# Order of the turned rows' parts, the place of the last turn, and the PSUM banks of the second down pass in a Griffin-style encoder layer

## The chip, the cores and the metric

The kernel runs on one core of a Trainium2 chip. The metric is the device time of one execution in microseconds (us); lower is better. One core has TensorE (matmuls; its rows in the profile are PE, and PEld for the loads of the stationary operand), VectorE (DVE), ScalarE (ACT), GpSimd (POOL) and SyncE (SP, which here issues DMAs). The on-chip memories are SBUF and PSUM; TensorE writes its results to PSUM, which has eight banks.

## The reference

One layer of a bidirectional hybrid encoder on 512 rows of 1024 float32 numbers. What matters here is its second half:

```python
x1 = x + rmsnorm(merged @ w_out, g_post_mix)
h2 = rmsnorm(x1, g_pre_ffn)
hid = conv3(h2 @ w_up) + conv_b            # w_up: 1024 x 5632, conv of width 3 along the rows
a, b = split(hid)                          # 2816 columns each
y = x1 + rmsnorm((gelu(a) * b) @ w_down, g_post_ffn)   # w_down: 2816 x 1024
```

The first half (a retention branch, a gated branch and their gates) makes `merged`; the change does not touch it.

## The kernel before, in words

**Precision.** Every matmul operand is held as two parts: a high part, which ScalarE copies into a reduced float32 type, and a low part, which VectorE makes by subtracting the high part from the original. A product is three matmuls: high by high, high by low, low by high. Where the original itself is needed later, a third copy, the raw rows, is made.

**Order.** The program is traced in Python, and a planner then puts the instructions of each engine in one fixed order at build time, from its own estimate of when each is ready, with earlier-traced ones first; it also hands out the buffers, PSUM banks among them, and sets the waits. So the order on an engine need not be that of the source. `tc.issue_after(ins)` forces instructions traced inside the block to stand behind `ins` on its engine. A PSUM bank is one tile from `ps()`; two engines' accesses to one bank are put one after the other, also when both only read.

**The turn.** `Down` computes `merged @ w_out` into eight accumulators, two for each of four row tiles t of 128 rows, and `finish(t, n)` adds the last six of eight blocks for one half n. `norms(t, acc)` makes the first norm and the residual x1 of row tile t, sends x1 out by DMA, and makes the rows of the second norm (`xn`, L873) from a scale (`row_scale`: L837 on DVE, L840 on POOL). `turn(t, zs)` transposes these rows on TensorE (L886, eight 128-column matmuls into two banks, one for each n), and evacuates each bank in two halves i: high parts (`h2h`, ACT), raw rows (`h2r`, ACT) and low parts (`h2l`, DVE, L892). Turns 0 and 1 fill group 0 (rows 0 to 255, the slice T0), turns 2 and 3 group 1 (T1).

Turn t-2 stands between the two `finish` calls of row tile t. After the loop, four blocks of the up projection start early: `early(e, 0)` is block e on T0 (24 matmuls of 256 columns, L219 to L221), `early(e, 1)` the same on T1. Turn 2 stands after `early(0, 0)`, turn 3 after `early(3, 0)`, right ahead of `early(0, 1)`, which is the first to read group 1. Then the rest of the up projection follows (plain blocks by L219 to L221, and a Strassen form of pairs by L673 that uses sums of the raw rows, L911 to L914), with conv and gate.

**The down projection** runs twice, once for each half of the 1024 output columns, in a Strassen-Winograd form: seven products M1, M2, M3, M5, M6, M7, M4 in this order, each in a PSUM bank of its own, accumulated over nine steps j; M8 is an eighth bank. In the last step of the first pass the `steps` functions combine the banks on VectorE into `c11` to `c22` as each product ends. The second pass takes new tiles from `ps()`, so each gets a bank of the first pass that has been read. On DVE the same stretch also holds the preparation of the next weights (L185, L189, L190 sums; L87 low parts `dl`).

Of the kernel before, what the change touches and what calls it, by code (L numbers as in the profile page):

```python
# [19 lines left out]
KD = D // P  # L20
# [28 lines left out]
def tile_block(ctx: ExitStack, tc, xT, x, wall, par, cs, wsp, bsp, gpost, gpre, gffn, out):  # L49
# [23 lines left out]
    def ps(shape=(P, S)):  # L73
        return pp.tile(list(shape), F32, tag="ps", name=nm("ps"))
# [4 lines left out]
    def copy(o, i):  # L79
        nc.scalar.activation(out=o, in_=i, func=AF.Copy)  # L80

    def as32(t):
        return t.bitcast(F32)
# [750 lines left out]
    def row_scale(q):  # L834

        s_, o = small("qs", 1, 4), small("qr", 1, 4)
        i = v.scalar_tensor_tensor(  # L837
            out=s_, in0=q[:, 0:1], scalar=EPS, in1=q[:, 1:2], op0=ALU.add, op1=ALU.add
        )
        nc.gpsimd.tensor_tensor(out=o, in0=s_, in1=nhalf[:, 0:1], op=ALU.pow)  # L840
        return o, i
# [7 lines left out]
    def norms(t, acc):  # L849

        xt = halves("x1")
        for n in range(2):
            nc.sync.dma_start(xt[n], x[t, :, n * S : (n + 1) * S])
        q = small("q", 2, 4)
        for n in range(2):
            mean_square(q, n, acc[n])
        sc, _ = row_scale(q)
        q = small("q", 2, 4)
        for n in range(2):
            z = tmp("z")  # L860
            v.scalar_tensor_tensor(
                out=z, in0=acc[n], scalar=sc, in1=gpm[n], op0=ALU.mult, op1=ALU.mult
            )
            v.tensor_add(xt[n], xt[n], z)
            mean_square(q, n, xt[n])
            nc.gpsimd.dma_start(x1[t][n], xt[n])
            if n == 0 and t in ADDED:
                nc.gpsimd.dma_start(out[t, :, 0:S], xt[0])
        sc, _ = row_scale(q)
        zs = []  # L870
        for n in range(2):
            z = tmp("xn")
            v.scalar_tensor_tensor(  # L873
                out=z, in0=xt[n], scalar=sc, in1=gpf[n], op0=ALU.mult, op1=ALU.mult
            )
            zs.append(z)
        return zs
# [2 lines left out]

    def turn(t, zs):
        g, c = t // 2, slice((t % 2) * P, (t % 2 + 1) * P)
        for n in range(2):
            p = ps()
            for f in range(4):
                nc.tensor.transpose(p[:, f * P : (f + 1) * P], zs[n][:, f * P : (f + 1) * P], ident)  # L886
            for i in range(2):
                hi, lo, raw = (h[g][2 * n + i].rearrange(two, i=2)[:, :, c] for h in (h2h, h2l, h2r))
                pf = p[:, 2 * i * P : 2 * (i + 1) * P].rearrange(two, i=2)
                copy(hi, pf)  # L890
                copy(raw, pf)
                v.tensor_sub(lo, pf, as32(hi))  # L892

    def h2(k, t):
        f = slice((k % 2) * 256, (k % 2 + 1) * 256)
# [19 lines left out]
        for n, t in zip(("S1", "S2", "S3", "S4"), (b1, a0, a1, b0)):  # L915
            h2_parts(n, i, t)

    def h2_block(w, o, q):
        wh, wl = w
        for k in range(KD):  # L920
            c = slice(k * P, (k + 1) * P)
            mm3(o[:, q], wh[:, c], wl[:, c], *h2(k, q), k == 0, k == KD - 1)

# [7 lines left out]

    early_w, early_o = [], []

    def early(e, q):

        if q == 0:
            early_w.append(w_get(1))
            early_o.append(ps())
        h2_block(early_w[e], early_o[e], (T0, T1)[q])

    dn_ = Down(mh, ml, KD, RES_OUT)
    zs = {}
    for t in range(NT):
        acc = [dn_.finish(t, 0)]
        if t > 1:
            turn(t - 2, zs[t - 2])
        acc.append(dn_.finish(t, 1))
        zs[t] = norms(t, acc)
    early(0, 0)
    turn(2, zs[2])  # L950
    for e in range(1, EARLY):
        early(e, 0)
    turn(3, zs[3])
    for e in range(EARLY):
        early(e, 1)

# [84 lines left out]
    def products(m, j, steps={}):  # L1041
        for n, (unit, at, act) in enumerate(UNITS):
            if n in (0, 3):
                wh, wl = w_get()
            if j == 0:
                m[n] = ps()
            f = slice(at * 256, (at + 1) * 256)
            ah, al = dforms[j][act]
            for t in range(2):
                c = slice(t * P, (t + 1) * P)  # L1050
                o = m[n][:, t * 256 : (t + 1) * 256]
                for i, (a_, w_) in enumerate(((ah, wh), (ah, wl), (al, wh))):
                    nc.tensor.matmul(  # L1053
                        o, a_[:, c], w_[:, f], start=j == t == i == 0,
                        stop=j == DP - 1 and i == 2 and n not in (M2, M3, M4), skip_group_check=True,
                    )
            steps.get(n, lambda: None)()
# [21 lines left out]
    c11, c12, c21, c22 = c4 = [blk(n="c") for _ in range(4)]  # L1079
    e1, e3, uu, yy = tmp("e1"), tmp("e3"), tmp("uu"), tmp("yy")  # L1080

    def after6():
        v.tensor_add(uu, m[M6], e1)
        v.tensor_sub(c12, m[M5], uu)
        v.tensor_add(c12, c12, e3)

    def after7():
        v.tensor_add(e1, m[M7], uu)
        v.tensor_sub(yy, m[M5], e1)  # L1089
        v.tensor_add(c22, c22, yy)  # L1090

    steps = {
        M1: lambda: copy(e1, m[M1]),
        M2: lambda: v.tensor_add(c11, m[M2], e1),
        M3: lambda: copy(e3, m[M3]),
        M6: after6, M7: after7,
        M4: lambda: v.tensor_add(c21, m[M4], e1),
    }
    for j in range(DP):
        if j < WHOLE:  # L1100
# [22 lines left out]
        v.tensor_add(qn[t][:, 0:1], qn[t][:, 2:3], qn[t][:, 3:4])  # L1123


    m = {}
    e1, uu, xx, yy = (blk(n="e") for _ in range(4))

    def after6():
# [10 lines left out]
        if 1 < j < 2 + NT:  # L1140
            first_share(j - 2)
    ww = [w_get(), w_get()]
    m[M8] = ps()

    def rows(t, sc, z, xt, some=(0, 1, 2)):

# [170 lines left out]
```

## Time and profile before

| | us |
|---|---|
| median of 3 runs | 829.89 |
| lowest and highest run | 827.95, 831.93 |
| the profiled execution, its own time | 832.1 |
| span of that execution, first to last instruction | 830.3 |
| PE busy in the span | 819.6 |
| PEld busy | 760.9 |
| DVE busy | 659.3 |
| ACT busy | 430.9 |
| POOL busy | 104.4 |

The mean granted TensorE clock is 0.998. Times in a timeline are counted from the span's start. A row of the timeline has the start, the duration, engine, line, operation, what is written from what, and in brackets the idle time of that engine before it and what ended it. TensorE is pipelined: a matmul's duration in a row is longer than the distance from its start to the next one's start, so the pace of TensorE is read from starts, or from the number of matmuls in a window.

### The profile page before, as it was taken

What the parts mean: (1) busy time and instruction counts of PE and PEld (TensorE: products, weight loads), DVE (VectorE), ACT (ScalarE), POOL (GpSimd) and SP (SyncE); (2) the same over time, 40 slices, a digit from 0 to 9 for tenths busy, and PEclk for the clock granted to TensorE, in tenths of its full rate; (3) what the DMA queues carried; (4) which work ended last, traced back from release to release, by engine and by line L of the source; (5) the groups of instructions that cost most, each with busy time, mean ns of one, the idle gap of its engine ahead of it and who ended that gap; (6) DMA issues with size and microseconds to landing.
All of it is one profiled execution on the core that took longest, in us unless ns stands there. A gap on an engine that the chain in (4) does not pass through costs nothing. (4 is left out here: it accounts for less than half of the span.)

```text
span 830.3 us, 14356 instructions
## 1 busy us (share of the span) xinstructions
PE 819.6 (99%) x5728; PEld 760.9 (92%) x5728; DVE 659.3 (79%) x1076; ACT 430.9 (52%) x733; POOL 104.4 (13%) x108
## 2 busy tenths in 40 slices
PE   9999999999999999999999999999999999999996
PEld 7888888888899999999988899999999999999995
DVE  7489898877897777767765679679899789997956
ACT  6635445546665444444444456456566566644532
POOL 0010000102221111133221201111111100000002
PEclk9999999999999999999999999999999999999999
DMA  8733222213233333233459121333323341243344
GB/s 279 258 115 104 75 77 77 76 52 99 69 102 126 102 102 93 87 100 102 121 178 349 64 67 37 105 104 99 116 91 101 110 147 50 77 141 103 115 128 127
DMA packets 29251, 93.84 MB, mean 113 GB/s; under 512 B 3392, under 2 KB 4032, under 8 KB 29184
## 3 DMA queue, kind: packets, MB, share of 16 engines
q1 hardware_dynamic: 26784, 86.58, 32.6%
q0 software_dynamic: 1968, 6.03, 2.3%
q8 instruction: 45, 0.74, 0.4%
q10 hardware_dynamic: 432, 0.30, 0.1%
q14 instruction: 22, 0.18, 0.1%
HBM read 88.19 MB, written 4.72 MB: 112 GB/s over the span
## 5 line engine op out<-in xcount | busy, mean ns | idle before, releaser
L87 DVE TENSOR_TENSOR wl<-raw,wh 128x1024 fp32r<-128x1024 f32 (+1 forms) x93 | 109.4, 1186 | 50.8 <-PE ps L673 27.3
L80 ACT ACTIVATE wf<-raw 128x512 fp32r<-128x512 f32 x140 | 85.3, 626 | 102.8 <-PE ps L220 45.0
L87 DVE TENSOR_TENSOR wf<-raw,wf 128x512 fp32r<-128x512 f32 x140 | 109.2, 795 | 26.8 <-ACT wf L80 25.9
L220 PE MATMUL ps<-h2l,wh 128*128 128x256 f32 x448 | 124.6, 279 | 0.2 <-DVE h2l L892 0.2
L219 PE MATMUL ps<-h2h,wh 128*128 128x256 f32 x448 | 123.7, 278 | 0.0
L221 PE MATMUL ps<-h2h,wl 128*128 128x256 f32 x448 | 123.7, 277 | 0.0
L673 PE MATMUL ps<-sh,wf 128*128 128x256 f32 x640 | 120.2, 277 | 0.1
L80 ACT ACTIVATE wh<-raw 128x1024 fp32r<-128x1024 f32 (+2 forms) x95 | 93.0, 989 | 35.9 <-DMA raw<-wall 13.3
L673 PEld LDWEIGHTS ps<-sh,wf 128*128 128x128 f32 x640 | 101.3, 188 | 0.8 <-DVE c L701 0.3
L673 PE MATMUL ps<-sl,wf 128*128 128x256 f32 x320 | 89.1, 278 | 0.0
L220 PEld LDWEIGHTS ps<-h2l,wh 128*128 128x128 f32 x448 | 83.9, 187 | 0.7 <-DVE h2l L892 0.7
L219 PEld LDWEIGHTS ps<-h2h,wh 128*128 128x128 f32 x448 | 83.8, 188 | 0.3 <-ACT h2h L80 0.3
L221 PEld LDWEIGHTS ps<-h2h,wl 128*128 128x128 f32 x448 | 83.9, 188 | 0.0
L481 PE MATMUL ps<-wh,xh 128*128 128x512 f32 x192 | 75.0, 391 | 0.0
L482 PE MATMUL ps<-wl,xh 128*128 128x512 f32 x192 | 74.9, 390 | 0.0
L483 PE MATMUL ps<-wh,xl 128*128 128x512 f32 x192 | 74.8, 390 | 0.0
L168 POOL TENSOR_TENSOR raw<-raw,raw 128x512 f32<-128x512 f32 x20 | 35.1, 1755 | 239.9 <-DVE raw L166 212.5
L1053 PE MATMUL ps<-dh,fh 128*128 128x256 f32 x216 | 60.9, 282 | 0.3 <-DVE yy L1089 0.2
L1053 PE MATMUL ps<-dh,fl 128*128 128x256 f32 x216 | 60.9, 282 | 0.0
L673 PEld LDWEIGHTS ps<-sl,wf 128*128 128x128 f32 x320 | 60.0, 188 | 0.3
L1053 PE MATMUL ps<-dl,fh 128*128 128x256 f32 x216 | 60.3, 279 | 0.0
L673 PE MATMUL ps<-xh,wf 128*128 128x256 f32 x288 | 54.4, 279 | 0.0
(309 smaller groups left out, 2040.1 us busy)
## 6 DMA issues: line engine op xcount, KB each, us to landing
raw<-wall SPq DMA_DIRECT2D x145, 512.0 KB, 3.6
x<-x SPq DMA_DIRECT2D x22, 256.0 KB, 5.5
xT<-xT SPq DMA_DIRECT2D x8, 256.0 KB, 5.4
x<-x POOLq DMA_DIRECT2D x8, 256.0 KB, 2.4
xT<-xT POOLq DMA_DIRECT2D x4, 256.0 KB, 3.8
out<-zs SPq DMA_DIRECT2D x3, 256.0 KB, 3.3
cs<-cs SPq DMA_DIRECT2D x2, 256.0 KB, 4.0
gpm<-gpost POOLq DMA_DIRECT2D x2, 256.0 KB, 3.8
```

The source lines that it names most:

```text
L80: nc.scalar.activation(out=o, in_=i, func=AF.Copy)
L87: nc.vector.tensor_sub(lo, src, as32(hi))
L168: nc.gpsimd.tensor_tensor(out=w_raw["T2"], in0=w_raw["T1"], in1=w_raw["B22"], op=ALU.add)
L219: nc.tensor.matmul(o, ah, bh, start=start, stop=False)
L220: nc.tensor.matmul(o, ah, bl, start=False, stop=False)
L221: nc.tensor.matmul(o, al, bh, start=False, stop=stop)
L481: nc.tensor.matmul(acc[t], xh[k][:, c], wh[:, f], start=k == 0, stop=False)
L482: nc.tensor.matmul(acc[t], xh[k][:, c], wl[:, f], start=False, stop=False)
L483: nc.tensor.matmul(acc[t], xl[k][:, c], wh[:, f], start=False, stop=k == KD - 1)
L673: nc.tensor.matmul(o, w_[:, c], a_, start=first and k == n == 0, stop=k == 3 and n == 2, skip_group_check=True,)
L1053: nc.tensor.matmul(o, a_[:, c], w_[:, f], start=j == t == i == 0, stop=j == DP - 1 and i == 2 and n not in (M2, M3, M4), skip_group_check= ...
```

## The change

Five edits:

1. In `turn`, the four raw copies on ScalarE are traced after all high and low parts of both banks, instead of each between its high and its low part; `turn` returns its last low part.
2. `norms` is split: its last part, the second scale and the two products by it (L837, L840, two L873), becomes `scaled(xt, q)`. For row tile 2 alone it is not traced at the end of `norms` but in the next round, after turn 1, and forced behind turn 1's last low part on DVE. For the other tiles it stays where it was. The DMAs of `norms` (x1, and part of the output) stay.
3. Turn 3 moves from the end of `early(3, 0)` to its middle, after 12 of its 24 matmuls.
4. In the first down pass, `c12 = M5 - uu` moves from after M6 to after M7, behind `yy = M5 - e1`; `c12 + e3` and `c22 + yy` move behind M4's `c21`.
5. The second pass gets its eight banks by name instead of from `ps()`: M1 the first pass's M8, M2 its M1, M3 its M2, M5 its M3, M6 its M6, M7 its M5, M4 its M7, M8 its M4.

```diff
@@ norms
             nc.gpsimd.dma_start(x1[t][n], xt[n])
             if n == 0 and t in ADDED:
                 nc.gpsimd.dma_start(out[t, :, 0:S], xt[0])
+        return xt, q
+
+    def scaled(xt, q):
         sc, _ = row_scale(q)
         zs = []
...
     def turn(t, zs):
         g, c = t // 2, slice((t % 2) * P, (t % 2 + 1) * P)
+        raws = []
         for n in range(2):
             p = ps()
...
                 copy(hi, pf)
-                copy(raw, pf)
-                v.tensor_sub(lo, pf, as32(hi))
+                low = v.tensor_sub(lo, pf, as32(hi))
+                raws.append((raw, pf))
+        for raw, pf in raws:
+            copy(raw, pf)
+        return low
...
-    def h2_block(w, o, q):
+    def h2_block(w, o, q, between=None):
         wh, wl = w
         for k in range(KD):
+            if between and k == KD // 2:
+                between()
             c = slice(k * P, (k + 1) * P)
             mm3(o[:, q], wh[:, c], wl[:, c], *h2(k, q), k == 0, k == KD - 1)
...
-    def early(e, q):
+    def early(e, q, between=None):
...
-        h2_block(early_w[e], early_o[e], (T0, T1)[q])
+        h2_block(early_w[e], early_o[e], (T0, T1)[q], between)
...
         if t > 1:
-            turn(t - 2, zs[t - 2])
+            low = turn(t - 2, zs[t - 2])
+        if t == 3:
+            with tc.issue_after(low.ins):
+                zs[2] = scaled(*xq)
         acc.append(dn_.finish(t, 1))
-        zs[t] = norms(t, acc)
+        xq = norms(t, acc)
+        if t != 2:
+            zs[t] = scaled(*xq)
     early(0, 0)
     turn(2, zs[2])
     for e in range(1, EARLY):
-        early(e, 0)
-    turn(3, zs[3])
+        early(e, 0, (lambda: turn(3, zs[3])) if e == EARLY - 1 else None)
...
-            if j == 0:
+            if j == 0 and n not in m:
                 m[n] = ps()
...
-    def after6():
-        v.tensor_add(uu, m[M6], e1)
-        v.tensor_sub(c12, m[M5], uu)
-        v.tensor_add(c12, c12, e3)
-
     def after7():
         v.tensor_add(e1, m[M7], uu)
         v.tensor_sub(yy, m[M5], e1)
+        v.tensor_sub(c12, m[M5], uu)
+
+    def after4():
+        v.tensor_add(c21, m[M4], e1)
+        v.tensor_add(c12, c12, e3)
         v.tensor_add(c22, c22, yy)
...
-        M6: after6, M7: after7,
-        M4: lambda: v.tensor_add(c21, m[M4], e1),
+        M6: lambda: v.tensor_add(uu, m[M6], e1), M7: after7, M4: after4,
...
-    m = {}
+    m = {n: m[o] for n, o in ((M1, M8), (M2, M1), (M3, M2), (M5, M3), (M6, M6), (M7, M5), (M4, M7), (M8, M4))}
...
-    m[M8] = ps()
```

## The prediction

> **What bounds the kernel now.** The page first, for the busiest engine; then the view of who waited for whom, for TensorE alone; then the timeline around each place that the change touches.
>
> ```profile
> span 830.3 us, 14356 instructions
> PE 819.6 (99%) x5728; PEld 760.9 (92%) x5728; DVE 659.3 (79%) x1076; ACT 430.9 (52%) x733; POOL 104.4 (13%) x108
> ```
>
> TensorE works 819.6 of 830.3 us, and no other engine comes near. So the time can change in two ways only: a gap between matmuls goes or comes, or the matmuls follow each other at another pace. The waits view shows nearly no gaps in the part that is changed:
>
> ```profile
> PE ps L1053 <- DVE yy L1089: 0.2, 1, 0.2
> PE ps L220 <- DVE h2l L892: 0.2, 1, 0.2
> ```
>
> These 0.2 us are the time in which no matmul was in flight. A matmul stays in flight for 0.28 us, while the next normally starts 0.11 to 0.12 us later, so a delay shorter than their difference leaves no idle time, and a longer one shows only in part. What a wait really costs must be read from the distance of starts. At the end of the turns before the early blocks:
>
> ```profile
> 469.95 0.37 ACT L80 ACTIVATE h2h<-ps 128x256 fp32r<-128x256 f32 x1
> 472.44 1.42 DVE L873 SCALAR_TENSOR_TENSOR xn<-x,qr,gpr 128x512 f32<-128x512 f32 x2 [0.74 <-POOL qr L840]
> 473.77 0.75 DVE L892 TENSOR_TENSOR h2l<-ps,h2h 128x256 fp32r<-128x256 f32 x2
> 474.22 0.39 ACT L80 ACTIVATE h2h<-ps 128x256 fp32r<-128x256 f32 x1 [1.32 <-DVE h2l L892]
> 474.91 0.98 DVE L892 TENSOR_TENSOR h2l<-ps,h2h 128x256 fp32r<-128x256 f32 x2 [0.40 <-ACT h2r L80]
> 473.94 0.28 PE L219 MATMUL ps<-h2h,wh 128*128 128x256 f32 x1
> 474.24 0.38 PE L220 MATMUL ps<-h2l,wh 128*128 128x256 f32 x1
> 474.46 0.28 PE L221 MATMUL ps<-h2h,wl 128*128 128x256 f32 x1
> 474.93 0.28 PE L219 MATMUL ps<-h2h,wh 128*128 128x256 f32 x1
> 475.39 0.39 PE L220 MATMUL ps<-h2l,wh 128*128 128x256 f32 x1 [0.18 <-DVE h2l L892]
> 475.61 0.28 PE L221 MATMUL ps<-h2h,wl 128*128 128x256 f32 x1
> ```
>
> Turn 1's first high part was there at 470.32, but its low part ran only at 473.77, after the two products of row tile 2's norm (472.44). TensorE wanted it at 474.05. The starts lie 0.30, 0.22, 0.46 and 0.22 us apart instead of 0.11: **0.75 us** lost.
>
> At turn 3, with turn 2 as the comparison (there nothing waits after the eight transposes):
>
> ```profile
> 477.44 1.04 PE L886 MATMUL ps<-ident,xn 128*128 128x128 f32 x8
> 478.24 0.36 PE L219 MATMUL ps<-h2h,wh 128*128 128x256 f32 x1
> 478.44 0.28 PE L220 MATMUL ps<-h2l,wh 128*128 128x256 f32 x1
> 486.88 1.03 PE L886 MATMUL ps<-ident,xn 128*128 128x128 f32 x8
> 487.79 0.38 ACT L80 ACTIVATE h2r<-ps 128x256 f32<-128x256 f32 x1
> 487.95 0.86 PE L219 MATMUL ps<-h2h,wh 128*128 128x256 f32 x5
> 488.20 0.98 DVE L892 TENSOR_TENSOR h2l<-ps,h2h 128x256 fp32r<-128x256 f32 x2 [3.43 <-ACT h2r L80]
> 488.64 0.43 PE L220 MATMUL ps<-h2l,wh 128*128 128x256 f32 x2
> 488.91 0.28 PE L221 MATMUL ps<-h2h,wl 128*128 128x256 f32 x1
> ```
>
> From the first transpose to the first matmul after them it is 1.07 us here against 0.80 there; the first of the five L219 takes 0.22, as the first after turn 2 does at 0.20, so 0.27 and 0.02 us; the two L220 take 0.27 instead of 0.24. **0.32 us** lost. The low part waits for the raw copy (487.79 to 488.17) ahead of it: its own bank, read by the other engine.
>
> At the change of passes:
>
> ```profile
> 765.59 0.41 DVE L190 TENSOR_TENSOR raw<-raw,raw 128x256 f32<-128x256 f32 x1
> 765.93 0.68 DVE L1084 TENSOR_TENSOR c<-ps,uu 128x512 f32<-128x512 f32 x1
> 766.53 1.22 DVE L87 TENSOR_TENSOR dl<-raw,dh 128x1024 fp32r<-128x1024 f32 x1
> 767.66 0.69 DVE L1085 TENSOR_TENSOR c<-c,e 128x512 f32<-128x512 f32 x1
> 768.26 0.69 DVE L1088 TENSOR_TENSOR e<-ps,uu 128x512 f32<-128x512 f32 x1
> 768.86 0.95 DVE L87 TENSOR_TENSOR dl<-raw,dh 128x768 fp32r<-128x768 f32 x1
> 769.73 0.69 DVE L1089 TENSOR_TENSOR yy<-ps,e 128x512 f32<-128x512 f32 x1
> 769.09 0.36 PE L1053 MATMUL ps<-dh,fh 128*128 128x256 f32 x1
> 769.29 0.28 PE L1053 MATMUL ps<-dl,fh 128*128 128x256 f32 x1
> 769.99 0.28 PE L1053 MATMUL ps<-dl,fa 128*128 128x256 f32 x1
> 770.47 0.39 PE L1053 MATMUL ps<-dh,fh 128*128 128x256 f32 x1 [0.19 <-DVE yy L1089]
> 770.69 0.28 PE L1053 MATMUL ps<-dl,fh 128*128 128x256 f32 x1
> ```
>
> DVE is in one unbroken queue here, and TensorE meets it twice. The matmul at 769.09 starts when L1088 ends (768.95), the last reader of old M7: 0.28 us late by the 0.12 pace, and 0.08 more to the next start, 0.36 us. The matmul at 770.47 starts when L1089 ends (770.42), the last reader of old M5: 0.36 and 0.11, **0.47 us**.
>
> **The change part by part.** The moved instructions are the same in number and form; what counts is what each delays.
>
> *Edits 1 and 2 at turn 1.* Without a raw copy between, a bank's chain is high 0.37, low 0.42, high, low. The first low can run when the DVE sum that ends at 470.7 is done; the other bank's follow, with ScalarE's mean square of the norm (0.63 and 0.19) in between. I estimate the last low by 473.1, against need at 474.05 for the first and 475.05 for the second: both waits go, −0.75 us. Bounds: −0.75, and 0 if the planner puts ScalarE's other work ahead and the lows stay late. I take −0.75, since the low's own predecessor was ready 3.4 us early. What is queued behind: row tile 2's scale on DVE and POOL and its two products (1.42) shift from 472.44 to about 474.1, ending at 475.5; no DMA is in the moved part, and POOL has nothing queued behind that scale until the next row tile's. Who waits: turn 2's transposes, wanted at 477.44 less 0.75, so 1.2 us of cover; without it each us late would be a us of TensorE. The four raw copies come later by about 1 us; their readers are the sums of the up pairs, far behind. Cost 0.
>
> *Edit 3.* Twelve matmuls of 0.119 stand between the transposes and the first reader: 1.4 us. By the rows above the first high and low need 0.38 + 0.42 after the fourth transpose, and the second pair of each bank 0.8 more while TensorE needs it 0.7 later: covered. Turn 3's rows must be ready 2.2 us earlier than now, at 484.7; the two products of row tile 3 follow 9 us after those of row tile 2, as the row tiles do, so by 483. The switch from transposes to matmuls (0.20 after the first, as at 478.24) is paid in either place. −0.32 us; bounds −0.32 and 0.
>
> *Edits 4 and 5.* M7 of the second pass now takes old M5's bank, whose last reader becomes `c12`, the third of three after `uu`; M4 takes old M7's, whose only reader is the first of the three. In the old queue five instructions stood between `uu` and the end of L1088: L190, L1084, L87 of 1024, L1085, L1088. In the new order I expect L190, L1088, L87 of 1024, L1089, L1084: as many, of the same lengths, ending at the same 768.95. So the 0.36 stays and the 0.47 goes. Bounds: −0.83 if no L87 stands between, and +0.40 if the L87 of 768 (0.87 from start to start) also gets ahead: −0.47 + 0.87. I take −0.47, for the count.
>
> Sum: −0.75 − 0.32 − 0.47 = **−1.54 us**. Against the profiled execution's 832.1 us (span 830.3 and 1.8 around it) that is 830.6; that execution was 2.2 above the median 829.89, so the median should come to **828.3 us**.
>
> **A pace that could eat it.** The same 256-column matmuls run at two paces:
>
> ```profile
> 479.00:486.00 7.00, 7.00 (x61) 7.00 (x60) 3.84 (x9) 3.24 (x12) 1.38 (x3) 1.00 0.19 75
> 500.00:600.00 100.00, 100.00 (x885) 100.00 (x884) 84.33 (x127) 56.86 (x96) 14.81 (x10) 1.00 0.29 90
> 641.00:695.00 54.00, 54.00 (x457) 54.00 (x456) 47.36 (x74) 32.37 (x53) 3.29 (x3) 1.00 0.36 108
> 637.74 0.34 PE L673 MATMUL ps<-h2h,wf 128*128 128x256 f32 x1
> ```
>
> In these windows (length, PE busy and number of matmuls first, granted clock 1.00 in all) a count takes in the matmuls in flight at the edge, so the pace is the length and 0.28 us, divided by the count: 0.1133 us from 500 to 600, 0.1188 from 641 to 695, on the same lines with the same kinds of operands, and 0.1193 after turn 2 (479 to 486). The changes come at disturbances: turn 2's transposes end the quick pace, the waits after turn 3 precede its return, a hesitation at 637.74 (a matmul in flight for 0.34 us) ends it. Which event leads to which pace the trace does not tell. If the quick pace does not come back after an undisturbed turn 3, 149 us by 0.1133, 1,315 matmuls, lose 0.0055 us each: 7.2 us, over four times the gain.
>
> The Trainium skill, "TensorE: Matmul & The Clock Gate", section "Back-to-back issue gap", puts an isolated gap at N/2.4 + 2.5 ns, 109 ns for 256 columns, and says that a stream's spacing is set by the weight load and the matmul together. By that alone there is one pace, no second one to fall into, and the sum stays −1.54 us; the trace shows 113 and 119 ns, neither of them 109, so it does not settle the rival.
>
> **The rivals.**
> - *The slow pace stays after turn 3* (slower). For it: turn 2, transposes without a wait behind them, was followed by the slow pace until the next event. Against: one example. 828.3 + 7.2 = 835.5 us. Some 280 matmuls (33 us) at the slow pace cancel the gain; 1,040 bring the time over 0.5%. Chance 0.26; 0.06 more that it lasts only part of the way, 830 to 833.
> - *The wait at the passes is only moved*: both L87 get ahead of `c12`. For it: the planner put both between dependent sums before. Against: by count only one is due. 828.3 + 0.87 = 829.2. Chance 0.1.
> - *The turn's lows stay late* behind ScalarE's mean squares, so edits 1 and 2 don't do what they say: 828.3 + 0.75 = 829.0. Chance 0.06.
> - *The quick pace lasts longer than before*, past 637.74, because the order there shifts: 72 us to the down passes, some 610 matmuls by 0.0055, −3.3: 825.0. Nothing in the edits aims at it. Chance 0.1.
>
> **How the numbers follow.** My forecast, 828.3, has the remaining 0.42; its own range is 826.5 to 830.2 (terms from −1.9 to 0 on the median, and the shown runs lie ±2 around theirs). A difference under 0.5%, 4.1 us, is about what a measurement of this kernel can tell from no change. Faster than 825.7: 0.1 from the last rival and a little from spread, less its misses, 0.11. Slower than 834.0: most of the first rival, 0.24. Within: 0.65. The range for 8 in 10 goes from 826.0 to 835.6, leaving out the faster rival and the top of the slow one.
>
> **What would show it.** Right: after turn 1 no L220 or L221 start is over 0.15 us after the last; DVE's low parts come ahead of row tile 2's L873; no gap at `early(0, 1)`; at the passes one late start near 769 less 1.1, none 1.4 us after it. Wrong: turn 2's transposes waiting for L873; both L87 ahead of L1084; and above all fewer than 870 matmuls per 100 us between 500 and 600.

## The result and the profile after

The changed kernel is slower, and outside the predicted range of 826.0 to 835.6 us.

| | median, us | lowest to highest | runs |
|---|---|---|---|
| before | 829.64 | 827.95 to 831.93 | 4 |
| after | 837.71 | 837.15 to 837.99 | 4 |

The ratio is 1.0083, with a 95% interval of 1.0063 to 1.0103. The waits that the edits aimed at are gone. What came in their place is not a wait: TensorE runs at its slower pace from turn 2 to the end of the up projection. This was the prediction's first rival; the time came out 2.2 us above the rival's 835.5. The profiled execution took 837.15 us (span 835.3). Its page:

```profile
span 835.3 us, 14346 instructions
PE 825.6 (99%) x5728; PEld 768.2 (92%) x5728; DVE 656.2 (79%) x1076; ACT 431.4 (52%) x733; POOL 104.1 (12%) x108
...
PE 97%; DVE 1%; issue 1%; POOL 1%; ACT 0%; POOLq 0%; DVEq 0%; ACTq 0%
```

The same 5,728 matmuls keep TensorE busy for 6.0 us longer (819.6 before), and the chain that ended last (the third line) lies on TensorE for 97% of the span. So no other engine holds it up; it is itself slower. The waits view of the same kernel has lost both rows that the prediction showed (`yy` at the passes, `h2l` at the turns):

```profile
PE ps L266 <- DVE raw L261: 1.0, 1, 1.0
PE ps L606 <- DVE o L616: 0.3, 1, 0.3
```

The windows of after (length, PE busy and number of matmuls first, granted clock third from the end), beside the prediction's windows of before:

```profile
479.00:485.00 6.00, 6.00 (x53) 6.00 (x52) 3.61 (x8) 3.10 (x11) 1.20 (x3) 1.00 0.23 89
500.00:600.00 100.00, 100.00 (x843) 100.00 (x842) 80.76 (x121) 52.75 (x89) 14.37 (x10) 1.00 0.28 90
641.00:695.00 54.00, 54.00 (x457) 54.00 (x456) 44.53 (x68) 32.16 (x52) 5.78 (x4) 1.00 0.35 108
```

From 500 to 600 there are 843 matmuls instead of 885: (100 + 0.28)/843 = 0.1190 us each instead of 0.1133. PE is busy for the whole window in both, so the busy share shows nothing; the count does. The granted clock is 1.00 in both, so it is not the clock.

How the difference builds up is seen by setting the n-th matmul of one trace against the n-th of the other (both have 5,728; in the middle of turn 3 alone the order differs). The table gives start in after less start in before, each from its span's start:

| place in before, us | after less before, us | what lies since the row above |
|---|---|---|
| 468 | −0.29 | start of the program |
| 480 | −1.05 | turns 1 and 2 |
| 500 | −0.85 | turn 3, then a short piece of up projection |
| 636 | +5.82 | up projection at the other pace |
| 645 | +5.51 | two waits of before at 637.74 and 639.45 that a slower TensorE doesn't meet |
| 709 | +5.51 | rest of up: slow in both of these traces |
| 765 | +5.51 | first down pass |
| 775 to the end | +4.92 | change of passes |

These two executions differ by 4.92 us. The medians differ by 8.07; the prediction's trace of before was 2.2 to 2.5 us above its median, and the run turn3_back_timed below suggests where: from 641 on.

### The profile page after: what moved, and what is told of

It is laid out like the page before. It is cut to its first block, busy times and chain, and to the rows that moved or that the text cites. A ratio compares the mean times of both kernels' runs of the same rounds, so it can differ in the third digit from the quotient of the medians.

```text
span 835.3 us, 14346 instructions
## 1 busy us (share of the span) xinstructions
PE 825.6 (99%) x5728; PEld 768.2 (92%) x5728; DVE 656.2 (79%) x1076; ACT 431.4 (52%) x733; POOL 104.1 (12%) x108
## 4 chain that ended last, share of the span: by engine, by line
PE 97%; DVE 1%; issue 1%; POOL 1%; ACT 0%; POOLq 0%; DVEq 0%; ACTq 0%
PE ps L673 24%; PE ps L220 13%; PE ps L219 13%; PE ps L221 12%; PE ps L1066 11%; PE ps L481 5%; PE ps L482 5%; PE ps L483 5%; PE ps L821 2%; PE ps L822 2%; PE ps L823 2%; PE ps L1083 2%; PE ps L746 1%; PE ps L281 1%; PE ps L266 0%
## 5 line engine op out<-in xcount | busy, mean ns | idle before, releaser
L87 DVE TENSOR_TENSOR wl<-raw,wh 128x1024 fp32r<-128x1024 f32 (+1 forms) x93 | 106.4, 1152 | 57.9 <-PE ps L673 31.2
L87 DVE TENSOR_TENSOR wf<-raw,wf 128x512 fp32r<-128x512 f32 x140 | 108.2, 788 | 31.5 <-ACT wf L80 30.8
L220 PE MATMUL ps<-h2l,wh 128*128 128x256 f32 x448 | 126.7, 283 | 0.0
L219 PE MATMUL ps<-h2h,wh 128*128 128x256 f32 x448 | 125.1, 279 | 0.0
L221 PE MATMUL ps<-h2h,wl 128*128 128x256 f32 x448 | 124.8, 278 | 0.0
L673 PE MATMUL ps<-sh,wf 128*128 128x256 f32 x640 | 121.5, 278 | 0.0
L673 PEld LDWEIGHTS ps<-sh,wf 128*128 128x128 f32 x640 | 101.9, 188 | 0.5 <-ACT u L80 0.2
L673 PE MATMUL ps<-sl,wf 128*128 128x256 f32 x320 | 89.7, 280 | 0.0
L219 PEld LDWEIGHTS ps<-h2h,wh 128*128 128x128 f32 x448 | 84.1, 188 | 0.0
L221 PEld LDWEIGHTS ps<-h2h,wl 128*128 128x128 f32 x448 | 84.0, 188 | 0.0
L220 PEld LDWEIGHTS ps<-h2l,wh 128*128 128x128 f32 x448 | 83.8, 187 | 0.0
L673 PEld LDWEIGHTS ps<-sl,wf 128*128 128x128 f32 x320 | 59.9, 187 | 0.3
L673 PE MATMUL ps<-xh,wf 128*128 128x256 f32 x288 | 54.4, 279 | 0.0
```

What stands on the lines that cost most here:

```text
L87: nc.vector.tensor_sub(lo, src, as32(hi))
L219: nc.tensor.matmul(o, ah, bh, start=start, stop=False)
L220: nc.tensor.matmul(o, ah, bl, start=False, stop=False)
L221: nc.tensor.matmul(o, al, bh, start=False, stop=stop)
L673: nc.tensor.matmul(o, w_[:, c], a_, start=first and k == n == 0, stop=k == 3 and n == 2, skip_group_check=True,)
```

## The experiments

**What was open.** The theory, A in the expectations: the two paces of the 256-column matmuls are states that keep themselves. Eight transposes with no wait behind them leave the slow one, a wait of TensorE in the plain blocks (L219 to L221) brings the quick one back, and edit 3 removed such a wait together with its 0.32 us. The rivals are in the expectations: another edit slows TensorE, or the loss comes from the order of the other engines. All extra matmuls below write into a PSUM bank just ahead of the block whose own first product overwrites it. A matmul is called late when it starts more than the usual 0.11 to 0.12 us after the one before it. Most runs are single executions, and runs of before spread over 4 to 5 us among themselves, so the pace in the trace carries each reading, more than the time.

**turn3_back: after without edit 3.**

```diff
-        early(e, 0, (lambda: turn(3, zs[3])) if e == EARLY - 1 else None)
+        early(e, 0)
+    turn(3, zs[3])
```

> The changed kernel with edit 3 alone undone: turn 3 stands again right ahead of the first block that reads it. Theory A (the pace of the 256-column matmuls has two self-keeping states, and the wait after turn 3 was what brought the quick one back): the wait of some 0.3 us returns, and with it over 870 matmuls per 100 us from 500 to 600; time 837.7 + 0.3 - 7 = about 831, or 828 where the quick pace lasts to the down passes. Theory B (the slow pace comes with something lasting in the changed kernel, its buffer places or its order on the other engines): the wait returns, the pace stays at 844 per 100 us, about 838.

It took 831.44 us in one run, beside 831.49 for before on the same chip. The wait is back (the first matmul after turn 3 starts 1.07 us behind the first transpose, as in before, where after has 0.79), and so is the quick pace behind it:

```profile
486.39 1.03 PE L890 MATMUL ps<-ident,xn 128*128 128x128 f32 x8
487.46 0.86 PE L219 MATMUL ps<-h2h,wh 128*128 128x256 f32 x5
500.00:600.00 100.00, 100.00 (x884) 100.00 (x884) 84.72 (x128) 57.01 (x96) 14.84 (x10) 1.00 0.27 90
641.00:695.00 54.00, 54.00 (x457) 54.00 (x456) 47.34 (x75) 32.25 (x52) 2.94 (x2) 1.00 0.33 108
```

So without edit 3 the loss is gone; edits 1, 2, 4 and 5 do not carry it by themselves. Five rounds of the same kernel follow further down.

**turn3_alone: before with edit 3 and nothing else.**

```diff
-        early(e, 0)
-    turn(3, zs[3])
+        early(e, 0, (lambda: turn(3, zs[3])) if e == EARLY - 1 else None)
...
```

> The kernel before with edit 3 alone: turn 3 in the middle of the last early block, all else as before. Theory A: no wait after turn 3, so the slow pace from there on, under 850 matmuls per 100 us from 500 to 600; time 829.6 - 0.3 + 7 to 9 = 836 to 838.5, with the two waits near 474 still there. Theory B: the quick pace stays, about 829.3.

832.38 us: the 836 to 838.5 of theory A was missed. The reason is in TensorE's timeline and the windows:

```profile
488.78 0.28 PE L219 MATMUL ps<-h2h,wh 128*128 128x256 f32 x1
489.05 0.39 PE L220 MATMUL ps<-h2l,wh 128*128 128x256 f32 x1
```

```profile
480.00:487.00 7.00, 7.00 (x62) 7.00 (x62) 3.19 (x8) 3.15 (x12) 1.10 (x2) 1.00 0.19 75
500.00:600.00 100.00, 100.00 (x885) 100.00 (x884) 84.27 (x124) 55.31 (x93) 14.30 (x10) 1.00 0.28 90
```

Here, where the raw copies still stand between the high and low parts (edit 1 is missing), one `h2l` matmul of turn 3 starts late after all, at 489.05, 0.27 us after the one before it. From 480 to 487 it is 7.28/62 = 0.117, with the eight transposes, which follow each other at 0.109, counted in; the matmuls around them are at 0.119, the slow pace. From 489.8 on it is quick (0.1133). The number was wrong because the wait was not gone; the pace did follow the wait. So edit 3 by itself does not lose the pace either: by these timelines the loss comes where the wait goes altogether, which in after takes the order of edit 1 as well.

**before_transposes: eight idle transposes in the quick stretch of before**, ahead of the sixth plain block after the early ones, at 532.9.

```diff
         w, o = w_get(), ps()
+        blocks[0] += 1
+        for i in range(8 if blocks[0] == 6 else 0):
+            f = slice((i % 4) * P, (i % 4 + 1) * P)
+            nc.tensor.transpose(o[:, f], ident, ident)
...
```

> The kernel before with eight added 128-column float32 transposes into a fresh bank (their result is overwritten) inside the quick stretch, ahead of the sixth up block after the early ones, near 545 us. Theory A: transposes without a wait behind them end the quick pace, as after turn 2: slow from there to 637, 92 us or 810 matmuls by 0.0055, +4.5, and +0.9 for the transposes: about 835. Theory B: the quick pace goes on, about 830.5.

```profile
500.00:530.00 30.00, 30.00 (x267) 30.00 (x267) 28.38 (x42) 17.05 (x28) 3.87 (x3) 1.00 0.26 87
540.00:600.00 60.00, 60.00 (x507) 60.00 (x506) 49.74 (x79) 34.16 (x59) 8.79 (x6) 1.00 0.32 106
```

837.54 us, against 831.49 for before on the same chip. The pace is 30.28/267 = 0.1134 ahead of them and 60.28/507 = 0.1189 behind them, until the up projection ends. The transposes take 0.9 us themselves (0.79 from the first to the matmul behind them, 0.09 to the next). The other 5.1 us fit the pace: the 104 us to 637.7 hold 918 matmuls at 0.1133, and each loses 0.0056. The expected 835 was counted on 829.6 and from 545 on. This shows the slow pace made on purpose, in the unchanged kernel, by transposes alone.

**after_wide12 and after_narrow24: extra matmuls ahead of the first plain block of after that follows turn 3.** Twelve of 512 columns in one, 24 of 256 columns in the other.

```diff
+        for _ in range(wide.pop() if wide else 0):       # wide = [12]
+            nc.tensor.matmul(o, w[0][:, 0:P], h2h[0][0], start=True, stop=True)
```
```diff
+        for _ in range(narrow.pop() if narrow else 0):   # narrow = [24]
+            nc.tensor.matmul(o[:, T0], w[0][:, 0:P], h2h[0][0][:, T0], start=True, stop=True)
```

> The changed kernel with twelve added 512-column matmuls into a fresh bank (their result is overwritten) ahead of the first up block after the early ones, near 512 us. In the kernel before the quick pace always follows upon 512-column matmuls. Theory A: quick pace from there to the down passes, about 199 us or 1,675 matmuls at 0.0055 us less, -9.2, and 12 x 0.227 = +2.7 for the added ones: about 831.2. Theory B: the pace stays slow, 837.7 + 2.7 = 840.4.

> Control for the twelve wide matmuls: the changed kernel with 24 added 256-column matmuls at the same place, the same columns in all. If it is the width that brings the quick pace (theory A): slow throughout, 837.7 + 24 x 0.119 = 840.6, under 850 matmuls per 100 us from 510 to 610. If any added work or the shift in time does it (rival): quick from there, about 833.4 as with the wide ones.

The windows of after_wide12, then of after_narrow24:

```profile
505.00:600.00 95.00, 95.00 (x840) 95.00 (x840) 75.98 (x114) 50.67 (x85) 14.85 (x10) 1.00 0.29 95
645.00:695.00 50.00, 50.00 (x423) 50.00 (x422) 43.34 (x69) 29.73 (x48) 2.94 (x2) 1.00 0.35 117
```

```profile
505.00:600.00 95.00, 95.00 (x801) 95.00 (x800) 74.62 (x112) 48.16 (x82) 13.10 (x9) 1.00 0.29 95
```

Twelve more wide matmuls, about 2.7 us of added work, make the kernel 4.3 us faster than after: 833.42 us. Behind them the pace is 95.28/840 = 0.1134. It is lost again at 641.29, behind an L673 matmul that starts 0.39 us after the one before it, which accounts for a time above theory A's 831.2. The 24 narrow ones do nothing: 95.28/801 = 0.1190, 841.05 us, near the expected 840.6. So added work does not help as such; the width does.

**after_waits: two waits made on purpose in after**, each by one more product whose result ScalarE copies away before the block's own first product may overwrite it: one ahead of the first plain block behind turn 3, one ahead of a pair of the L673 form.

```diff
+        if blocks[0] == 1:
+            mm3(o[:, T0], w[0][:, 0:P], w[1][:, 0:P], *h2(0, T0), True, True)
+            copy(probe, o[:, 0:16])
...
+            if probe is not None:                        # the pair i == 8
+                nc.tensor.matmul(o, wh[:, 0:P], act(0)[0], start=True, stop=True, skip_group_check=True)
+                copy(probe, o[:, 0:16])
```

> The changed kernel with two added waits and no wide matmul: in the first up block after the early ones (plain form, L219 to L221) three extra matmuls and a small ScalarE copy of their bank, which the block's own first matmul has to wait for; and one extra matmul with such a copy at the start of the third couple's first product (the form of L673). So far waits in the plain form were followed by the quick pace and waits in the form of L673 by the slow one. If a wait alone is enough in the plain form: quick from about 500 to the second wait near 560, slow after it, 837.7 + 1.5 - 2.9 = 836.3. If a wait alone does nothing: slow throughout, about 839.

```profile
506.00:560.00 54.00, 54.00 (x479) 54.00 (x478) 40.04 (x60) 26.72 (x45) 8.95 (x6) 1.00 0.27 90
570.00:630.00 60.00, 60.00 (x507) 60.00 (x506) 51.12 (x80) 35.73 (x61) 8.80 (x6) 1.00 0.33 103
```

```profile
563.52 0.39 PE L676 MATMUL ps<-h2h,wf 128*128 128x256 f32 x1 [0.36 <-ACT probe L80]
```

835.2 us. A late start in the plain form at 498.82 (0.27 us after the one before it) is followed, 6 us later, by the quick pace (54.28/479 = 0.1133). A wait in the L673 form (here L676) at 563.52 ends it (60.28/507 = 0.1189). So "a wait brings the quick pace" is too simple: it also matters in which form the wait falls. This fits the end of the quick pace of before, from 637.74 to 639.45, also in L673. The length of the wait does not explain it: in before the L220 matmul at 475.39 starts 0.46 us after the one before it and leaves the pace quick (0.113 to 0.114 from 476.1 on), the one of L673 at 639.45 starts 0.35 us after and ends it. What differs between the forms, operands or something else, no run separates.

**places: where do wide matmuls help?** Six ahead of an earlier pair of the first half, three ahead of the first plain block behind turn 3, six ahead of a pair of the L673 form, meant for 640, and twelve at the start of the first down pass.

```diff
+            for _ in range(wide):
+                nc.tensor.matmul(
+                    self.b[b], wh[:, 0:P], xh[0] if self.act is x_act else h2h[0][0],
+                    start=True, stop=True, skip_group_check=True,
+                )
...
```

> The changed kernel with wide matmuls at four places, a different number at each: 6 at the second u pair (near 223 us), 3 at the first up block after the early ones (near 497), 6 at the sixth couple (near 640), 12 at the start of the first down pass (near 709). What each number does is read from the pace behind it. In the kernel before, six to twelve wide ones pass before their own pace has settled at 0.227 us, so I expect 12 and 6 to be enough and 3 to be doubtful. All four working: 837.7 + 27 x 0.227 - 1.8 (u pairs) - 10 (up) - 4 to 5 (down, both passes) = 827.5; with the down passes unable to run quick, 832.

```profile
505.00:600.00 95.00, 95.00 (x840) 95.00 (x840) 77.53 (x117) 51.00 (x86) 14.83 (x10) 1.00 0.28 95
645.00:695.00 50.00, 50.00 (x423) 50.00 (x422) 41.83 (x66) 28.73 (x47) 2.94 (x2) 1.00 0.34 116
716.00:760.00 44.00, 44.00 (x376) 44.00 (x375) 37.57 (x63) 22.00 (x30) 0.59 (x1) 1.00 0.31 102
```

837.24 us, above both expected numbers (827.5 and 832). Three in the plain form are enough (0.1134). The six meant for 640 ran at 623.93 to 625.31, where the pace was quick before and behind them, so they tell nothing; a wait at 640.64, of 0.37 us, is followed by the slow pace (50.28/423 = 0.1189). The down pass stays at 44.28/376 = 0.1178 right behind its twelve. The earlier pair stayed slow (0.119 from 226 to 262), but its six ran as two groups of three, at 222.5 and 224.7.

**wide12_aligned, offsets_40, offsets_32, offsets_48: the places of the operands in SBUF.** In the up blocks of both kernels the high weights lie 48 words into their slot and the low ones 16; in the down passes it is 16 and 48. These runs put both parts at the same word: 0 in up (with the twelve wide matmuls) in wide12_aligned; 40 in up and 24 in down; 32 and 32; 48 and 16.

```diff
-                (slot("wh", 48), slot("wl", 16)) if i >= UP0 else (slot("wh"), slot("wl"))
+                (slot("wh", 40), slot("wl", 40)) if i >= UP0 else (slot("wh"), slot("wl"))
...
```

> The changed kernel with the twelve wide matmuls, and the weight slots of the up projection starting at word 0 instead of at words 48 and 16, so that weights and moving rows start alike in a group of 64 words, as in the score products near 70 to 190 us, which run at 0.120 us per matmul right behind wide ones. If the quick pace needs the two operands' addresses apart (theory A2): slow after the wide ones too, 840 to 842. If addresses have no part in it: quick after them, 833.4.

> The changed kernel with other places inside the weight slots, nothing else: in the u pairs and the up projection high and low parts both start at word 40 of a group of 64 (before: 48 and 16), in the down passes both at word 24 (before: 16 and 48). In the slow pace the matmul beside which a low part at word 16 is loaded is in flight longest (283 ns against 278 and 279), and alike starts gave 120 ns whatever stood ahead. If the slow pace is a meeting of the weight load's and the moving operand's reads, that the distance of their starts governs, a distance nearer to half of 64 should leave the quick pace alone: 113 ns in the u pairs, the up projection and perhaps the down passes: 837.7 - 1.5 - 12 = 824, and 820 with the down passes. If the distance matters only where it is zero: as the changed kernel, 837.7.

> The same with word 32 for all of them. By the meeting of reads, with the load starting some 3 ns (about 7 words) after the matmul, 32 leaves less on one side than 40: quick or mixed, 824 to 838. If only zero matters: 837.7.

> The same with word 48 for high and low parts of the u pairs and the up projection, and 16 for both in the down passes: the places of the changed kernel, without the two that look worst (low parts at 16, down low parts at 48). If it is the low parts' place that keeps the slow pace up: quick, 824. If not: 837.7.

One window each, in this order:

```profile
505.00:600.00 95.00, 95.00 (x794) 95.00 (x793) 74.63 (x112) 48.04 (x81) 12.88 (x9) 1.00 0.28 95
```
```profile
500.00:600.00 100.00, 100.00 (x836) 100.00 (x835) 83.07 (x125) 54.82 (x91) 11.50 (x8) 1.00 0.28 91
```
```profile
500.00:600.00 100.00, 100.00 (x845) 100.00 (x844) 83.69 (x126) 54.66 (x90) 12.34 (x9) 1.00 0.29 95
```
```profile
500.00:600.00 100.00, 100.00 (x852) 100.00 (x851) 82.88 (x125) 54.33 (x92) 13.11 (x10) 1.00 0.27 91
```

The paces are 0.1200, 0.1200, 0.1187 and 0.1177 us, the times 842.41, 846.3, 842.32 and 837.03. None reaches 0.1133, in wide12_aligned not even behind wide matmuls. Of the expected numbers only those of wide12_aligned (840 to 842, slow) and offsets_48 (837.7, not quick) came about, near enough; offsets_40 and offsets_32 were slower than both of theirs, and the meeting of reads that they were to test is not confirmed. So the pace depends on where the two weight parts lie.

**turn3_back_timed and turn3_back_wide3: five rounds.** The first is turn3_back again. The second adds three wide matmuls at 648, behind the place where the L673 waits end the quick pace.

```diff
+        for _ in range(3 if blocks[0] == 17 else 0):
+            nc.tensor.matmul(o, w[0][:, 0:P], h2h[0][0], start=True, stop=True)
```

> The changed kernel with edit 3 undone, timed against the kernel before in five rounds. Both show the quick pace from 488 to 637 in single looks, so what is left is edits 1, 2, 4 and 5: the prediction has them at -0.75 and -0.47, so 1.2 us faster, ratio 0.9985. If they bring nothing (their waits only come back elsewhere): ratio 1.000.

> The same kernel with three wide matmuls at the start of the first plain up block behind the waits near 639, after which the pace has been slow so far. Three were enough in the plain form near 497. If so here: quick from 641 to the down passes, 65 us or 550 matmuls by 0.0055, -3.0, and +0.7 for the three: 2.3 us less than without them, ratio to the kernel before about 0.996. If TensorE at the quick pace runs into VectorE again there and loses it in the form of L673: between that and 0.7 us more than without them.

turn3_back_timed: 828.36 us (826.72 to 830.98, 12 runs) against 829.57 (827.0 to 832.21, 23 runs), ratio 0.9986 with a 95% interval of 0.997 to 1.0003: 1.2 us less, as expected, though the interval takes in no change. Its profiled execution, of 828.05 us, differs above all in one window from the first execution of the same kernel, at 831.44:

```profile
641.00:695.00 54.00, 54.00 (x479) 54.00 (x478) 49.72 (x80) 33.05 (x53) 2.94 (x2) 1.00 0.36 118
```

479 matmuls from 641 to 695 instead of 457: here the quick pace came back after the same L673 waits. By the n-th matmul this execution is 0.51 us ahead at 636 and 3.75 ahead at 709, so the stretch is worth 3.2 us, of which a late VectorE (`dl`, L87) takes 0.76 back at 722.89. So most of the difference between these two executions goes with whether the pace returns there.

turn3_back_wide3 took 829.21 us, ratio 1.0001 (0.9987 to 1.0015), where about 0.996 was expected. In its trace the three do what they should:

```profile
641.00:648.00 7.00, 7.00 (x62) 7.00 (x61) 6.99 (x12) 5.45 (x9) 0.00 (x0) 1.00 0.53 186
652.00:695.00 43.00, 43.00 (x382) 43.00 (x381) 36.69 (x61) 25.13 (x40) 2.94 (x2) 1.00 0.33 105
```

The pace ahead of them is 7.28/62 = 0.117 by the coarse count of a short window (0.119 from start to start), and 43.28/382 = 0.1133 behind them. But the kernel without them can be quick there by itself, and the 12 runs with them still spread from 828.53 to 831.59. So what the rest of the spread comes from stays open.

**offsets_swapped, swapped_timed, before_swapped: the two places exchanged**, high at 16 and low at 48 in the up blocks and the pairs, 48 and 16 in the down passes. The first two are the same kernel, after with the exchange; the third is before with the exchange and none of the five edits.

```diff
-            hi, lo = (slot("wh", 16), slot("wl", 48)) if i >= DOWN0 else (
-                (slot("wh", 48), slot("wl", 16)) if i >= UP0 else (slot("wh"), slot("wl"))
+            hi, lo = (slot("wh", 48), slot("wl", 16)) if i >= DOWN0 else (
+                (slot("wh", 16), slot("wl", 48)) if i >= UP0 else (slot("wh"), slot("wl"))
...
-        hi, lo = w[:, S + 48 : 2 * S + 48], w[:, 16 : S + 16]
+        hi, lo = w[:, 16 : S + 16], w[:, S + 48 : 2 * S + 48]
...
-        hi, lo = slot("dh", 16, w), slot("dl", 48, w)
+        hi, lo = slot("dh", 48, w), slot("dl", 16, w)
```

> The changed kernel with the places in the weight slots exchanged: in the u pairs and the up projection high parts at word 16 and low ones at 48, in the down passes the other way round. Equal places for high and low parts (32, 40, 48) had no quick pace anywhere, the changed kernel's 48 and 16 have it between the wide matmuls from 264 to 430. If it needs only that the two differ: quick from 264 to 430 as before, and slow behind turn 3, 837.7. If it needs this order of the two: slow from 264 to 430 as well, some 840, and perhaps quick in the down passes, where the changed kernel's order never had it, -4.

> The changed kernel with the places of high and low weights in their slots exchanged (high at word 16 and low at 48 in the up blocks, 48 and 16 in the down passes). Theory: with this placing the quick pace of 0.1133 us survives turn 3 without any wait, so the changed kernel keeps its four removed waits and the pace: 825 to 826.5 us, a ratio of 0.995 to 0.997, about 880 matmuls per 100 us between 500 and 600. Rival: the single look at 825.8 was luck, and the pace falls off in most executions: 831 to 838 us, 1.000 to 1.010.

> The kernel before with the same exchange of places and none of the five edits. Theory: the pace is quick here with or without the waits, and the waits of turn 1, turn 3 and the change of passes remain, so it is about 1.5 us (the sum of the prediction) above the changed kernel with the exchange: 826.5 to 828 us, a ratio of 0.996 to 0.998 to the kernel before. Rival: the exchange shortens something else that the edits touch, and the two come out alike, or the edits still cost with the exchange: this one below the other.

| five rounds on one chip | median, us | lowest to highest | ratio to before, 95% |
|---|---|---|---|
| before (11 runs) | 831.43 | 829.18 to 832.65 | |
| before_swapped (6 runs) | 827.15 | 826.84 to 827.71 | 0.9952 (0.9939 to 0.9965) |
| swapped_timed (6 runs) | 825.44 | 824.93 to 825.65 | 0.993 (0.9916 to 0.9944) |

The run offsets_swapped took 825.8 us. This fits neither expectation of that run (837.7 or some 840, perhaps with 4 less for quick down passes); the theory of the other two was made from it. Their expected times hold (825 to 826.5 and 826.5 to 828), while the ratios came out a little lower than expected, since before took 831.43 here; the rivals' numbers do not hold. With the exchange the pace is quick with or without the waits. The timeline and windows of swapped_timed:

```profile
474.60 1.04 PE L890 MATMUL ps<-ident,xn 128*128 128x128 f32 x8
475.39 0.36 PE L219 MATMUL ps<-h2h,wh 128*128 128x256 f32 x1
475.59 0.28 PE L220 MATMUL ps<-h2l,wh 128*128 128x256 f32 x1
```

```profile
477.00:482.00 5.00, 5.00 (x47) 5.00 (x46) 3.38 (x8) 2.10 (x9) 1.44 (x3) 1.00 0.28 107
500.00:600.00 100.00, 100.00 (x885) 100.00 (x884) 84.02 (x127) 55.52 (x94) 14.86 (x10) 1.00 0.30 97
641.00:695.00 54.00, 54.00 (x479) 54.00 (x478) 49.65 (x79) 33.31 (x54) 2.94 (x2) 1.00 0.33 112
```

Turn 2's transposes, with no wait behind them, are now followed by 5.28/47 = 0.112 us, by the coarse count of a short window, where both given kernels have 0.119; the up projection is quick to its end (54.28/479 = 0.1133). The down passes keep their 0.118. With the pace out of the way the five edits show their own worth, 827.15 − 825.44 = **1.71 us** between runs that do not overlap; the prediction's sum was 1.54. By the n-th matmul, swapped_timed against before_swapped, it is 0.75 at turns 1 and 2 (468 to 480), 0.37 around turn 3 (480 to 500) and 0.67 at the passes (730 to 775). The version with the edits and the exchange beats both given kernels.

## Why the prediction was wrong, and where it was right

Its own steps, by the profile of after:

```profile
470.67 0.42 DVE L895 TENSOR_TENSOR h2l<-ps,h2h 128x256 fp32r<-128x256 f32 x1
471.87 0.76 DVE L895 TENSOR_TENSOR h2l<-ps,h2h 128x256 fp32r<-128x256 f32 x2 [0.79 <-ACT h2h L80]
473.30 0.42 DVE L895 TENSOR_TENSOR h2l<-ps,h2h 128x256 fp32r<-128x256 f32 x1 [0.67 <-ACT h2h L80]
474.53 1.42 DVE L876 SCALAR_TENSOR_TENSOR xn<-x,qr,gpr 128x512 f32<-128x512 f32 x2 [0.74 <-POOL qr L840]
473.66 0.28 PE L219 MATMUL ps<-h2h,wh 128*128 128x256 f32 x1
473.77 0.28 PE L220 MATMUL ps<-h2l,wh 128*128 128x256 f32 x1
484.40 1.03 PE L890 MATMUL ps<-ident,xn 128*128 128x128 f32 x8
485.19 0.36 PE L219 MATMUL ps<-h2h,wh 128*128 128x256 f32 x1
485.39 0.28 PE L220 MATMUL ps<-h2l,wh 128*128 128x256 f32 x1
771.38 0.68 DVE L1096 TENSOR_TENSOR e<-ps,uu 128x512 f32<-128x512 f32 x1
771.98 1.21 DVE L87 TENSOR_TENSOR dl<-raw,dh 128x1024 fp32r<-128x1024 f32 x1
773.11 0.68 DVE L1097 TENSOR_TENSOR yy<-ps,e 128x512 f32<-128x512 f32 x1
773.71 0.68 DVE L1098 TENSOR_TENSOR c<-ps,uu 128x512 f32<-128x512 f32 x1
774.20 0.28 PE L1066 MATMUL ps<-dh,fl 128*128 128x256 f32 x1
774.45 0.39 PE L1066 MATMUL ps<-dh,fh 128*128 128x256 f32 x1
774.67 0.28 PE L1066 MATMUL ps<-dl,fh 128*128 128x256 f32 x1
```

- **Turn 1, −0.75: right.** The low parts (now L895) run from 470.67, and the first `h2l` matmul starts 0.11 after the one before it. The table has −0.29 to −1.05, so −0.76. The last low part ends at 473.72, not 473.1, still in time. The two products for row tile 2 (now L876) end at 475.95, not 475.5; turn 2's transposes do not wait.
- **Turn 3, −0.32: right.** From the first transpose to the first matmul behind them it is 0.79 instead of 1.07, and 0.20 to the next, with no second delay.
- **Passes, −0.47: right in kind, a little better in size.** VectorE's order is the expected one, with one `L87` between: `e` (L1096), `L87` of 1024, `yy`, `c12` (L1098). The kept wait at 774.45 is 0.25 − 0.12 and 0.22 − 0.12, so 0.23 us instead of 0.36, and the table has −0.59. There is no late start 1.4 us after it. The rivals "only moved" and "lows stay late" did not happen.
- **The pace: the step that failed.** The prediction saw the two paces, named edit 3's wait as a candidate for the return of the quick one, and priced its loss at 7.2 us over 149 us. It then gave that 0.26, because turn 2 was "one example", took the return of the quick pace as likelier, and so put the pace at nothing in its sum of −1.54. Measured, this term was +6.67 us from 500 to 636 alone. The trace of before held one case of each: turn 3's transposes, with a wait behind them, were followed by the quick pace, and turn 2's, without, by the slow one. No row showed the quick pace behind transposes without a wait. The runs turn3_back, before_transposes and after_waits show that this was the rule for the weights' given places, and swapped_timed that it is not for the exchanged ones. The price itself was right: 6.67 us in 136 are 0.049 for each us, 7.3 over 149.
- **The range.** The rival's 835.5 missed 837.71 by 2.2. Its 7.2 us were read from one trace of before, slow from 641 to 709, and added to a sum on the median, 2.2 us lower; from that execution itself the sum is 830.6 + 7.2 = 837.8, close to what came. A kernel with the wait can be quick in that stretch (turn3_back_timed: 3.2 us, 2.5 after VectorE's late part), and the median of before probably holds some of that, which no trace of a faster execution of before shows; in all four runs of after, within 0.84 us of each other, no such gain appears. The prediction noted that its execution lay 2.2 above the median and did not ask in which stretch.

The Trainium skill, "TensorE: Matmul & The Clock Gate", section "Back-to-back issue gap", has the spacing of a stream set by the weight load and the matmul; by that alone there is one spacing for one shape, and the rival could not happen. Here the same shapes ran at 0.1133, 0.1177, 0.119 and 0.120 us at a granted clock of 1.00, so the measurement decides.

## What to carry to other kernels

When one engine is busy for all of its span, count its instructions in equal windows of the trace: a second, slower pace of one shape is a cost that neither the busy share nor the waits view shows, and here 5% of pace over 136 us outweighed all four removed waits. Before removing a wait, look what follows each place where that wait is and is not; a state that the wait resets belongs in the sum, and one example for it, with none against, deserves more than one chance in four. When runs of a kernel spread over more than the gain in question, find the stretch in which they differ before setting one execution against the median.

## What the runs showed of the hardware

The quick and the slow pace differ little in one matmul. The groups view of 505 to 595, before and then after (mean ns behind the busy time):

```profile
L220 PE MATMUL ps<-h2l,wh 128*128 128x256 f32 x161 | 44.4, 276 | 0.0
```
```profile
L220 PE MATMUL ps<-h2l,wh 128*128 128x256 f32 x153 | 43.3, 283 | 0.0
```

An L220 matmul is in flight for 276 ns at the quick pace and 283 at the slow one (L219 and L221: 276, against 279 and 278), and the distance between starts is 113 and 119 ns. With the high weights at word 48 and the low ones at 16 both paces keep themselves: 128-column transposes with no wait behind them, or a wait in the L673 form, were followed by the slow one (the wait in 7 traces of 8, turn3_back_timed being the exception), and a wait in the plain form or three 512-column matmuls ahead of a plain block by the quick one. Not every 128-column matmul does what the transposes do: in before the sixteen of L746 that end near 279.6, with no wait behind them, are followed by the quick pace (4.28/38 = 0.113 from 281 to 285, in the L673 form). With 16 and 48 the quick pace is not disturbed, in swapped_timed neither by the transposes nor by a late start in L673 at 635.84. With both at one word it was never reached (0.1177 to 0.120), and the down passes stayed between 0.1177 and 0.120 in every run. What in the chip does this stays open: that places in SBUF matter points to the reading of the two operands, but no run measured that by itself.
